# Four pads that shift SBUF buffers by 128 to 384 bytes in a two-layer hybrid encoder

## The chip, the cores and the metric

The kernel runs on one core of a Trainium2 chip. The metric is the device time of one execution, in microseconds (us). Every run of the kernel before took between 1643.23 and 1654.07 us, with a median of 1650.0 us over three runs. TensorE is called PE in the rows, and its weight loads PEld; VectorE is DVE, ScalarE is ACT, GpSimd is POOL, and SP is the queue that issues most transfers.

## The reference

The reference is an encoder trunk of two layers on 512 positions of width 1024, in float32. Layer 0 mixes with dilated window attention and chunked gated linear attention; layer 1 mixes with a bidirectional state-space layer and a convolution module. Each layer then has cross-attention into 256 memory tokens and a gated feed-forward block with a depthwise convolution of width 3:

```python
def reference(...):
    h = x
    for layer in range(DEPTH):              # DEPTH = 2
        i = layer // 2
        hn = rmsnorm(h, g_mix[layer])
        if layer % 2 == 0:
            h = h + mixer_ab(hn, ...)        # attention and gated linear attention
        else:
            h = h + mixer_cd(hn, ...)        # S5 state space and Conformer convolution
        memn = rmsnorm(mem, g_mem[layer])
        h = h + cross_attention(rmsnorm(h, g_xattn[layer]), memn, ...)
        h = h + conv_ffn(rmsnorm(h, g_ffn[layer]), ...)
    return rmsnorm(h, g_final)

def conv_ffn(hn, w_up, w_conv, b_conv, w_down):
    u = depthwise_conv(hn @ w_up, w_conv, b_conv)      # width 1024 -> 2 * 2816
    val, gate = jnp.split(u, 2, axis=-1)
    return (jax.nn.silu(gate) * val) @ w_down          # width 2816 -> 1024
```

Nearly all of the arithmetic is in dense products: the projections of the mixers, the four of the cross-attention, and `w_up` and `w_down`.

## The kernel before

**Activations.** Features lie on the 128 partitions and the 512 positions along the free axis. The residual stream is eight tiles `h[c]`, each 128x512 float32. To keep float32 accuracy, each operand of a dense product is held as two parts of type float32r: `hg[c]`, 128x2x512, holds the high part of the normed stream in `hg[c][:, 0]` and what is left of it in `hg[c][:, 1]`. The same shape is used for the outputs of the mixers (`oa`, `ob`, and `cm`, `at`, `bm`, `cst` in layer 1), of the cross-attention (`ox`), and for the gated product of the feed-forward block (`g`).

**Weights.** A block of weights, 128x1024 float32, is brought by one DMA into `wr` (line 140). ScalarE copies it to `wh` as float32r (line 194), and VectorE (GpSimd for some blocks, lists `LPOOL` and `XPOOL`) computes the rest `wl` (line 195). Then TensorE runs, for each of the block's eight chunks of 128 columns, three matmuls (`mm3`, lines 199 to 201): high by high, high by low, low by high. Each of them loads 128x128 weights into the array and streams a moving operand of 512 columns past them. So a block is 24 matmuls, and each of these has a weight load of its own; PE's instructions come in the fixed sequence load, matmul, load, matmul.

**Order of work.** A scheduler lays out the instructions of each engine when the kernel is built. In the mixers and the cross-attention PE's order is also pinned by hand (`pinned`, `XSEQ`, `CD`), and small float32 matmuls and transposes stand between the blocks. In the feed-forward block (`ffn`) the order is `up` for the 22 chunk pairs and `down` for three groups of them (`GROUPS`), almost all of it full blocks: `up` has `hg` as moving operand, `down` has `g`. During layer 0's feed-forward block GpSimd and VectorE also compute parameters of layer 1's state-space part (`tick`, `s5_params`).

**Buffers.** SBUF is given out by pools in the order in which the pools and their tiles are opened: `P` ("keep") for what lives throughout, `WP` for `wr`, `wh` and `wl`, and one pool for each stage (`T`, `TG`, `TA`, `TM`, `TP`). A tile that is allocated earlier moves the later ones of the same side up by its size. In the program as built, `hg` starts in each partition at a place that leaves 480 when divided by 512 bytes, and the weight buffers `wh` and `wl` leave 352. Chunks within a block and halves within a tile lie 512 or 2048 bytes apart, so that the remainder is the same for a whole buffer. The remainders of the others stand in the table in the section on the change. "Distance" below is the start of the weights that are loaded beside a matmul, less the start of that matmul's moving operand, modulo 512 bytes: for `hg` with `wh` it is 352 - 480 = 384.

Of the kernel before, what the change touches and what calls it, by code (L numbers as in the profile page):

```python
# [11 lines left out]
F32 = mybir.dt.float32  # L12
# [78 lines left out]
def trunk(ctx, tc, xT, memT, pos, vec, amask, cmask, bmask,  # L91
# [4 lines left out]
    P = ctx.enter_context(tc.tile_pool(name="keep", bufs=1))  # L96
# [6 lines left out]
    def nm(p):  # L103
        n_[0] += 1
        return f"{p}_{n_[0]}"
# [15 lines left out]

    h = [P.tile([128, S], F32, tag=f"h{c}", bufs=1, name=f"h{c}") for c in range(NC8)]
    hg = [P.tile([128, 2, S], F32R, name=f"hg{c}") for c in range(NC8)]

    def mm_ps():
        return PS.tile([128, 512], F32, tag="mm", bufs=4, name=nm("mm"))
# [71 lines left out]
    def mm3(ps, lH, lL, rH, rL, start, stop):  # L198
        PE.matmul(ps, lH, rH, start=start, stop=False)  # L199
        PE.matmul(ps, lH, rL, start=False, stop=False)  # L200
        PE.matmul(ps, lL, rH, start=False, stop=stop)  # L201
# [96 lines left out]
    def mixer_ab(nnext, eskv):  # L298
        es = ExitStack()
        T = es.enter_context(tc.tile_pool(name="m0", bufs=1))  # L300

        def b2(tag, bufs, pool=None):
            return (pool or T).tile([128, S], F32, tag=tag, bufs=bufs, name=nm(tag))
# [405 lines left out]
        TM = es.enter_context(tc.tile_pool(name="m0m", bufs=1, side="right"))  # L709
        mg = [TM.tile([128, 2, S], F32R, name=f"mg{i}") for i in range(4)]  # L710
        TA = es.enter_context(tc.tile_pool(name="m0a", bufs=1))
        o_a = [TA.tile([128, 2, S], F32R, name=f"oa{i}") for i in range(4)]
        def ptrans(t, j, p_):
            tp = tp_ps()
            for jt in range(4):
                PE.transpose(tp[:, 128 * jt:128 * jt + 128], p_[:, 128 * jt:128 * jt + 128], ident)  # L716
            pt = b2("pt", 3, TA)
            if j % 2 == 0:
                A.activation(pt, tp, AF.Copy)
            else:  # L720
                V.tensor_copy(pt, tp)
            return pt

        def pv(t, j, pt):
# [6 lines left out]
            if j == 7:  # L731
                den = pair[t][1]
                V.reciprocal(den, den)
                on = b2("on", 1, TA)
                V.tensor_tensor(on.rearrange("p (j d) -> p j d", d=64), onat.rearrange("p (j d) -> p j d", d=64),
# [210 lines left out]
    def ffn(l, norm, nnext, start=None, tick=lambda n: None):  # L946
# [3 lines left out]
        if start is not None:  # L950
            start()
# [108 lines left out]
    def s5_angles(T):  # L1060

        def sm(tag):
            return T.tile([128, 64], F32, name=nm(tag))

        lam = T.tile([128, 3, 64], F32, name="lam")
        nc.sync.dma_start(lam, s5v)
        lr, li, dt = lam[:, 0], lam[:, 1], lam[:, 2]
        tact(dt, dt, AF.Exp)
        x, th, den, t1, t2, t3 = sm("x"), sm("th"), sm("den"), sm("t1"), sm("t2"), sm("t3")
        mul(x, lr, dt)  # L1070
        mul(th, li, dt)
        mul(den, lr, lr)
        mul(t1, li, li)
        add(den, den, t1)
        V.reciprocal(den, den)

        tact(t1, x, AF.Tanh, scale=0.5)
        G.tensor_scalar(t2, t1, -1.0, 1.0, op0=ALU.mult, op1=ALU.add)
        V.reciprocal(t2, t2)
        mag, em1 = sm("mag"), sm("em1")  # L1080
        G.tensor_scalar(mag, t1, 1.0, None, op0=ALU.add)
        mul(mag, mag, t2)
        G.tensor_scalar(em1, t1, 2.0, None, op0=ALU.mult)
        mul(em1, em1, t2)

        G.tensor_scalar(t1, th, 1.0 / TWO_PI, MAGIC, op0=ALU.mult, op1=ALU.add)
        G.tensor_scalar(t1, t1, -MAGIC, None, op0=ALU.add)
        for cst in (PI2_A, PI2_B, PI2_C):
            G.tensor_scalar(t2, t1, -cst, None, op0=ALU.mult)
            add(th, th, t2)  # L1090
        G.tensor_scalar(th, th, PI_F, -PI_F, op0=ALU.min, op1=ALU.max)
        sn, cs, c1 = sm("sn"), sm("cs"), sm("c1")
        tact(sn, th, AF.Sin)
        tact(c1, th, AF.Sin, scale=0.5)
        A.activation(t1, th, AF.Abs)
        tact(cs, t1, AF.Sin, scale=-1.0, bias=hpi_c)
        return sm, lr, li, x, th, den, t1, t2, t3, mag, em1, sn, cs, c1
# [152 lines left out]
    def mixer_cd(norm, nnext, kv):  # L1250
        es = ExitStack()
        T = es.enter_context(tc.tile_pool(name="m1", bufs=1))
# [15 lines left out]
        for j in range(2):  # L1268
            G.memset(vg[j][:, :, 0:2], 0.0)
            G.memset(vg[j][:, :, 66:68], 0.0)  # L1270
        uT, At, Rg, X, cm, tab, rot = {}, {}, {}, {}, {}, {}, {}

        part, done_ = {}, set()
# [304 lines left out]
    def dump():  # L1578
        for c in range(NC8):
            nc.sync.dma_start(out[c], h[c])  # L1580

    n1 = Norm("g_xattn0")
    eskv = ExitStack()
    kv0 = mixer_ab(n1, eskv)
    if upto == 0:
        return dump()
# [6 lines left out]
    with tc.tile_pool(name="s5p", bufs=1) as TP:  # L1593
        angles, todo, clock = [], [], [0]

        def start():
            angles.append(s5_angles(TP))
            todo.append(s5_params(TP, angles[0]))

        def tick(n):  # L1600

            clock[0] += n
            if clock[0] >= S5_EVERY:
                clock[0] -= S5_EVERY
                next(todo[0], None)

        ffn(0, n2, n3, start, tick)
        for _ in todo[0]:
            pass
        if upto == 2:  # L1610
            return dump()
    n4 = Norm("g_xattn1")
    eskv = ExitStack()
    kv1 = KV(1, eskv)
    mixer_cd(n3, n4, kv1)
    if upto == 3:
        return dump()
# [106 lines left out]
```

## Time and profile before

| | us |
|---|---|
| median of three runs | 1650.0 |
| lowest and highest run | 1643.23, 1654.07 |
| the profiled execution | 1640.53 |
| span of its trace, first to last instruction | 1638.7 |
| PE busy in the span | 1585.5 (97%) |
| PEld busy | 1308.6 (80%) |
| DVE, ACT, POOL busy | 1081.1, 708.1, 366.4 |

The time outside the span is 1.8 us. The mean granted clock of TensorE is 0.988 of the full 2.4 GHz. The profile shows a matmul from its start to its modelled end, and the next one starts before that end; so the mean duration of a matmul (398 ns for those of 512 columns with `hg`) is not what one of them costs in a stream. What one costs is the step from a start to the next start: the length of an undisturbed stretch divided by the matmuls that start in it.

### The profile page before, as it was taken

Reading aid. Unit: us, or ns where it says so; the run is one execution under the profiler, and the core shown is the slowest. Engines: PE = TensorE matmul, PEld = TensorE weight load, DVE = VectorE, ACT = ScalarE, POOL = GpSimd, SP = SyncE. Lnnn points to the kernel's source line nnn. Section 1 sums busy time; section 2 is a strip of 40 time slices with the busy share of each in tenths; the row PEclk is TensorE's granted clock in tenths of the full one; section 3 lists DMA queues with packets and bytes.
Section 4 is the critical chain, followed back from the end, with each engine's and each line's share of the span. In section 5 each row is a group of like instructions: output and inputs, shape, how many; then the busy total and the mean of one; then the engine's idle time right before and its main releaser. Section 6 shows DMA issues by size and latency. Waiting matters only on the chain.

```text
span 1638.7 us, 20958 instructions
## 1 busy us (share of the span) xinstructions
PE 1585.5 (97%) x8036; PEld 1308.6 (80%) x8036; DVE 1081.1 (66%) x1475; ACT 708.1 (43%) x1089; POOL 366.4 (22%) x371
## 2 busy tenths in 40 slices
PE   8999999999999999999999899989999999999997
PEld 6788889888877777877887777878888888888887
DVE  7576766466578899389655997275745766636644
ACT  6464755344444433234335233364534434414423
POOL 8411000000079844444500101230000101100101
PEclk9999999999999999999999899999999999999999
DMA  5322334131222335435544573542302323332231
GB/s 175 108 76 91 117 95 138 52 116 52 74 90 78 121 122 161 135 109 169 148 147 150 181 280 121 201 172 88 103 29 81 100 94 100 90 102 91 82 112 64
DMA packets 76117, 189.11 MB, mean 115 GB/s; under 512 B 8368, under 2 KB 27440, under 8 KB 76016
## 3 DMA queue, kind: packets, MB, share of 16 engines
q1 hardware_dynamic: 75376, 186.58, 35.4%
q8 instruction: 63, 1.03, 0.3%
q0 software_dynamic: 320, 1.05, 0.2%
q14 instruction: 38, 0.31, 0.1%
q10 hardware_dynamic: 320, 0.13, 0.0%
HBM read 162.43 MB, written 19.01 MB: 111 GB/s over the span
## 4 chain that ended last, share of the span: by engine, by line
PE 73%; DVE 12%; POOL 6%; issue 3%; ACT 3%; DMA 3%; SPq 1%; DVEq 0%; ACTq 0%; POOLq 0%
PE mm L201 20%; PE mm L199 20%; PE mm L200 20%; DVE wl L195 2%; PE mm L729 2%; DVE t L963 1%; PE sc L1480 1%; DVE dv L1454 1%; DVE t L964 1%; PE tp L1365 1%; PE tp L716 1%; DVE u L960 1%; POOL t L1131 1%; DVE t L968 1%; POOL wl L195 1%
## 5 line engine op out<-in xcount | busy, mean ns | idle before, releaser
L194 ACT ACTIVATE wh<-wr 128x1024 fp32r<-128x1024 f32 (+1 forms) x229 | 238.9, 1044 | 432.6 <-PE mm L200 349.4
L201 PE MATMUL mm<-hg,wl 128*128 128x512 f32 x1000 | 397.7, 398 | 13.0 <-DVE wl L195 12.6
L199 PE MATMUL mm<-hg,wh 128*128 128x512 f32 x1000 | 402.4, 402 | 0.3 <-ACT wh L194 0.3
L200 PE MATMUL mm<-hg,wh 128*128 128x512 f32 x1000 | 397.1, 397 | 0.0
L195 DVE TENSOR_TENSOR wl<-wr,wh 128x1024 fp32r<-128x1024 f32 (+1 forms) x215 | 279.7, 1301 | 69.6 <-ACT wh L194 67.6
L201 PEld LDWEIGHTS mm<-hg,wl 128*128 128x128 f32 x1000 | 189.5, 190 | 62.6 <-DVE wl L195 16.1
L199 PEld LDWEIGHTS mm<-hg,wh 128*128 128x128 f32 x1000 | 189.6, 190 | 46.8 <-issue 2.2
L200 PEld LDWEIGHTS mm<-hg,wh 128*128 128x128 f32 x1000 | 189.4, 189 | 44.7 <-issue 1.2
L201 PE MATMUL mm<-g,wl 128*128 128x512 f32 x324 | 127.5, 394 | 2.2 <-DVE wl L195 2.2
L199 PE MATMUL mm<-g,wh 128*128 128x512 f32 x324 | 127.9, 395 | 0.0
L200 PE MATMUL mm<-g,wh 128*128 128x512 f32 x324 | 127.2, 392 | 0.0
L968 POOL TENSOR_TENSOR t<-t,t 128x512 f32<-128x512 f32 x22 | 29.0, 1318 | 431.7 <-ACT t L175 431.7
L960 DVE TENSOR_TENSOR u<-mm,R 128x512 f32<-128x512 f32 x88 | 60.3, 687 | 81.5 <-PE mm L201 81.4
L962 ACT ACTIVATE t<-u,vt 128x512 f32<-128x512 f32 x88 | 71.1, 810 | 52.3 <-DVE u L960 52.0
L978 DVE TENSOR_TENSOR h<-mm,h 128x512 f32<-128x512 f32 x40 | 27.6, 690 | 90.7 <-PE mm L201 90.7
L963 DVE SCALAR_TENSOR_TENSOR t<-u,vt,t 128x511 f32<-128x511 f32 x88 | 77.7, 883 | 3.8 <-ACT t L962 3.8
L964 DVE SCALAR_TENSOR_TENSOR t<-u,vt,t 128x511 f32<-128x511 f32 x88 | 76.7, 872 | 4.0 <-DMA dct<-tr 1.4
L201 PEld LDWEIGHTS mm<-g,wl 128*128 128x128 f32 x324 | 60.9, 188 | 16.6 <-DVE wl L195 2.8
L175 ACT ACTIVATE t<-t 128x512 f32<-128x512 f32 x44 | 27.8, 632 | 101.3 <-DVE t L964 101.3
L200 PEld LDWEIGHTS mm<-g,wh 128*128 128x128 f32 x324 | 60.9, 188 | 13.4
L199 PEld LDWEIGHTS mm<-g,wh 128*128 128x128 f32 x324 | 60.9, 188 | 13.2
L195 POOL TENSOR_TENSOR wl<-wr,wh 128x1024 fp32r<-128x1024 f32 x14 | 35.0, 2504 | 136.6 <-ACT wh L194 111.8
(522 smaller groups left out, 3036.4 us busy)
## 6 DMA issues: line engine op xcount, KB each, us to landing
wr<-in_w_up SPq DMA_DIRECT2D x88, 512.0 KB
wr<-in_w_dn SPq DMA_DIRECT2D x32, 448.0 KB
wr<-in_w_ab SPq DMA_DIRECT2D x16, 512.0 KB
wr<-in_w_xv SPq DMA_DIRECT2D x16, 512.0 KB
wr<-in_w_xk SPq DMA_DIRECT2D x16, 512.0 KB
wr<-in_w_xq SPq DMA_DIRECT2D x16, 512.0 KB
wr<-in_w_xo SPq DMA_DIRECT2D x16, 512.0 KB
wr<-in_w_dn SPq DMA_DIRECT2D x16, 512.0 KB
```

Of the source, the lines that this page charges most:

```text
L175: tabbed(A.activation(dst, src, fn, **kw))
L194: A.activation(H[:, :n], raw[:, :n], AF.Copy)
L195: (eng or V).tensor_tensor(L[:, :n], raw[:, :n], H[:, :n].bitcast(F32), ALU.subtract)
L199: PE.matmul(ps, lH, rH, start=start, stop=False)
L200: PE.matmul(ps, lH, rL, start=False, stop=False)
L201: PE.matmul(ps, lL, rH, start=False, stop=stop)
L729: PE.matmul(onat[:, 64 * j:64 * j + 64], pt[:, 128 * jt:128 * jt + 128], va[:, jt, 64 * hd:64 * hd + 64], start=jt == 0, stop=jt == 3)
L960: V.tensor_tensor(u, ps, R, ALU.mult)
L962: A.activation(t, u, AF.Identity, scale=vc(f"cw{l}", 44 + i), bias=vc(f"cb{l}", i))
L963: V.scalar_tensor_tensor(t[:, 1:], u[:, :S - 1], vc(f"cw{l}", i), t[:, 1:], op0=ALU.mult, op1=ALU.add)
L964: V.scalar_tensor_tensor(t[:, :S - 1], u[:, 1:], vc(f"cw{l}", 88 + i), t[:, :S - 1], op0=ALU.mult, op1=ALU.add)
L968: (V if l == 0 else G).tensor_tensor(res[1], res[1], res[0], ALU.mult)
```

## The change

A helper `pad` allocates a tile of so many bytes in a partition and leaves it unused. It is called four times: 128 bytes in `P` after `hg`, 384 bytes in `TA` ahead of `oa`, 192 bytes in the pool of `mixer_cd`, and 320 bytes in `TP`, which lies ahead of the feed-forward tiles of layer 0. No instruction reads or writes a pad.

```diff
     h = [P.tile([128, S], F32, tag=f"h{c}", bufs=1, name=f"h{c}") for c in range(NC8)]
     hg = [P.tile([128, 2, S], F32R, name=f"hg{c}") for c in range(NC8)]
+
+    def pad(pool, n):
+        pool.tile([128, n // 4], F32, name=nm("pad"))
+
+    pad(P, 128)
...
         TA = es.enter_context(tc.tile_pool(name="m0a", bufs=1))
+        pad(TA, 384)
         o_a = [TA.tile([128, 2, S], F32R, name=f"oa{i}") for i in range(4)]
...
             G.memset(vg[j][:, :, 66:68], 0.0)
+        pad(T, 192)
         uT, At, Rg, X, cm, tab, rot = {}, {}, {}, {}, {}, {}, {}
...
             angles.append(s5_angles(TP))
             todo.append(s5_params(TP, angles[0]))
+            pad(TP, 320)
```

On all five engines the instructions stand in the same order, name for name, and wait for the same semaphores as before. What differs is where buffers start. The starts modulo 512 bytes, from the two programs as built:

| buffer | role in a matmul of 512 columns | before | changed |
|---|---|---|---|
| `hg` | moving; weights in `natural` | 480 | 480 |
| `wh`, `wl`, and `xh`, `xl` of the cross-attention | weights; moving in `natural` and `vstep` | 352 | 480 |
| `mg` | weights | 480 | 480 |
| `g`, layer 0 | moving | 32 | 480 |
| `g`, layer 1 | moving | 352 | 480 |
| `ob`, `ox` | moving | 352 | 480 |
| `oa` | moving | 480 | 480 |
| `cm`, `at`, `bm`, `cst` | moving | 160 | 480 |
| `pT` with weights `vn` | moving, weights | 480, 480 | 96, 96 |

PE's order has 5395 places at which a float32r matmul of 512 columns is followed by the weight load of another one. Counted by distance they are:

| distance | 0 | 128 | 192 | 256 | 320 | 384 |
|---|---|---|---|---|---|---|
| before | 1052 | 389 | 144 | 0 | 567 | 3243 |
| changed | 5373 | 10 | 0 | 8 | 0 | 4 |

## Rows read from the trace of the kernel before

**Rows 1.** The page: span, busy time of each engine, share of the last chain.
```profile
span 1638.7 us, 20958 instructions
PE 1585.5 (97%) x8036; PEld 1308.6 (80%) x8036; DVE 1081.1 (66%) x1475; ACT 708.1 (43%) x1089; POOL 366.4 (22%) x371
...
PE 73%; DVE 12%; POOL 6%; issue 3%; ACT 3%; DMA 3%; SPq 1%; DVEq 0%; ACTq 0%; POOLq 0%
```

**Rows 2.** The page's costliest groups: matmuls with hg and g; busy, mean, idle before.
```profile
L199 PE MATMUL mm<-hg,wh 128*128 128x512 f32 x1000 | 402.4, 402 | 0.3 <-ACT wh L194 0.3
L200 PE MATMUL mm<-hg,wh 128*128 128x512 f32 x1000 | 397.1, 397 | 0.0
...
L199 PE MATMUL mm<-g,wh 128*128 128x512 f32 x324 | 127.9, 395 | 0.0
```

**Rows 3.** Timeline in layer 1's feed-forward block: start, duration, engine, line, operation.
```profile
1425.69 0.40 PE L199 MATMUL mm<-hg,wh 128*128 128x512 f32 x1
1425.69 0.19 PEld L200 LDWEIGHTS mm<-hg,wh 128*128 128x128 f32 x1
1425.92 0.39 PE L200 MATMUL mm<-hg,wh 128*128 128x512 f32 x1
1425.93 0.19 PEld L201 LDWEIGHTS mm<-hg,wl 128*128 128x128 f32 x1
```

**Rows 4.** PE by stretch: from:to, length, busy (matmuls), granted clock, DMA share, GB/s.
```profile
418.86:451.77 32.91, 32.91 (x146) 1.00 0.31 97
459.62:531.25 71.63, 71.63 (x308) 1.00 0.27 89
830.22:864.52 34.30, 34.30 (x148) 1.00 0.48 156
1265.60:1426.59 160.99, 160.99 (x691) 1.00 0.30 95
1426.59:1470.13 43.54, 43.54 (x193) 1.00 0.31 97
1470.13:1548.53 78.40, 78.40 (x337) 1.00 0.28 91
1548.53:1601.13 52.60, 52.60 (x233) 1.00 0.36 106
```

**Rows 5.** The same view of three short streams.
```profile
54.00:59.10 5.10, 5.10 (x23) 1.00 0.30 103
67.40:78.09 10.69, 10.69 (x47) 1.00 0.44 113
411.07:415.85 4.78, 4.78 (x22) 1.00 0.00 0
```

**Rows 6.** Groups by shape on PE over the whole span.
```profile
L200 PE MATMUL mm<-wl,hg 128*128 128x512 f32 x64 | 25.9, 405 | 0.7 <-DVE wl L195 0.7
...
L201 PE MATMUL mm<-wh,hg 128*128 128x512 f32 x64 | 25.0, 394 | 0.0
...
L199 PE MATMUL mm<-wh,hg 128*128 128x512 f32 x64 | 24.4, 404 | 0.2 <-ACT wh L194 0.2
...
L200 PE MATMUL mm<-pT,vn 128*128 128x512 f32 x24 | 9.0, 389 | 0.0
```

**Rows 7.** PE by stretch: two streams of matmuls of 256 columns.
```profile
249.44:252.05 2.61, 2.61 (x24) 1.00 0.33 126
...
1606.20:1619.51 13.31, 13.31 (x113) 1.00 0.01 1
```

**Rows 8.** All engines by stretch: length, PE, PEld, DVE, ACT, POOL busy, granted clock.
```profile
560.00:650.00 90.00, 83.72 (x377) 67.13 (x375) 81.51 (x104) 36.62 (x53) 46.40 (x28) 0.98 0.45 135
710.00:790.00 80.00, 73.43 (x333) 59.19 (x332) 74.50 (x98) 31.82 (x47) 38.24 (x23) 0.98 0.44 134
870.00:950.00 80.00, 72.68 (x372) 59.94 (x371) 64.08 (x92) 32.80 (x51) 7.45 (x4) 0.91 0.53 184
950.00:1050.00 100.00, 89.89 (x585) 76.48 (x585) 65.23 (x87) 36.30 (x55) 16.67 (x7) 0.97 0.55 190
```

**Rows 9.** Who waited for whom: waits in us, times, longest.
```profile
PE mm L201 <- DVE wl L195: 15.4, 9, 3.8
```

## The prediction

> **What bounds the kernel.** I read the engines' busy time and the chain of waits first. PE is busy for 1585.5 of 1638.7 us, and 73% of the chain that ended last is PE work [rows 1]. The costliest groups are dense matmuls of 512 columns, three lines of 1000 each with `hg` and of 324 each with `g` as moving operand [rows 2], and PE waited for nothing ahead of most of them. So the price of one such matmul in a stream sets the time. The mean durations of 395 to 402 ns [rows 2] are not that price, since a matmul begins before the modelled end of the one before. The timeline shows the step: starts at 1425.69 and 1425.92, and the load of the next weights begins within 10 ns of each matmul [rows 3]. What PE reads together is therefore a matmul's moving operand and the weights of the next.
>
> **The step depends on the distance, in the trace of before.** I took undisturbed stretches, all at granted clock 1.00, the full 2.4 GHz, and divided each by its matmuls [rows 4]. The count of each stretch holds one matmul that began ahead of its left edge, so one is taken off.
>
> - `hg` in three stretches, distance 384: 71.63/307, 160.99/690 and 78.40/336 us, 233.3 ns each time.
> - `g` in layer 0, distance 320: 34.30/147, 233.3 ns.
> - `g` in layer 1, distance 0: 43.54/192 and 52.60/232, 226.8 and 226.7 ns.
> - `ox` in the cross-attention, distance 0: 32.91/145, 227.0 ns.
>
> The two stretches of `g` do the same work from the same weight buffers, and differ in where the moving operand lies. In layer 1 `hg` and `g` alternate four times without a pause, and the step goes 233.3, 226.8, 233.3, 226.7. The DMA share, 0.27 to 0.48, doesn't sort them: it is 0.36 in the stretch of 226.7 and 0.28 in one of 233.3. So the change's claim is visible before it is made: 6.5 ns less per matmul at distance 0, in a long stream.
>
> **The change, part by part.** No instruction is added, removed or moved. The pads' effect is on distances: of 5395 places where one matmul of 512 columns follows another, 4343 have a distance other than 0 now, and 22 afterwards. At some 150 of the 4343 PE waits for something first, and I count no gain there: 4193 are left.
>
> *Long streams.* The four of [rows 4] at distance 384 or 320 hold 307 + 690 + 336 + 147 = 1480 matmuls. At 6.5 ns: 9.6 us.
>
> *The other 2713* stand in shorter streams, between small matmuls, transposes and waits. Short streams of `hg` now take 5.10/22 = 231.8 and 10.69/46 = 232.4 ns; a short one of `ox` at distance 0 takes 4.78/21 = 227.6 ns [rows 5]. So one gains 4.2 to 4.8 ns in streams as short as these and 6.5 in long ones. I take 5.2, nearer to the short end, because most of these streams are 20 to 50 matmuls: 14.1 us. The upper bound is 6.5 (17.6 us). The lower is 3, if the streams between waits are too broken to settle (8.1 us).
>
> *The 1052 places at distance 0 now* stay there: nothing. *Matmuls of 256 columns* (`mg` moving, 384 of them) go from distance 384 to 0 too. A stream at 384 takes 2.61/22 = 118.6 ns and one at 0 takes 13.31/111 = 119.9 [rows 7] (here two began early), so these lose 1.3 ns each, about 0.5 us. *Small float32 matmuls and transposes* change distance as well; the half-width ones bound them at 1.3 ns for the some 1900 that are left, 2.5 us either way, and I take 0.
>
> *What is hidden again.* A gain ahead of a wait for another engine is lost if that engine doesn't get faster. In two stretches of layer 0's feed-forward block DVE is busy for 81.51 of 90 and 74.50 of 80 us, and PE waits [rows 8]; the waits of PE for DVE's `wl` are 15.4 us in all, at 9 places [rows 9]. Some 550 of the 4193 matmuls lie in those stretches, 2.9 us of gain at 5.2 ns. In the state-space mixer, 870 to 1120 us, PE also has holes and the granted clock is 0.91 and 0.97 in [rows 8]; 440 matmuls, 2.3 us. If all of it is absorbed, 5.2 us; I take half, 2.6, because DVE's work on each chunk starts from a PE result and moves forward with it.
>
> Sum: 9.6 + 14.1 - 0.5 - 2.6 = 20.6 us. Bounds: 9.6 + 8.1 - 0.5 - 5.2 - 2.5 = 9.5 and 9.6 + 17.6 - 0.5 + 2.5 = 29.2. The profiled execution took 1640.5 us, of which 1638.7 is span; it would take 1619.9. It stands 9.5 below the median of the runs shown, 1650.0, and under the lowest of them. I expect the gain to be the same in every run, since it sits in each matmul: **1629.4 us**, 1.25% faster.
>
> **A rule that speaks against it.** The rows show 233.3 and 226.8 ns for the same work at two places of its operand [rows 4]. The Trainium skill, page "TensorE: Matmul & The Clock Gate", section "Part 2: What happens when you issue a matmul", says that TensorE has two independent read ports into SBUF, so that loading the next weights takes no read bandwidth from the running matmul. By that, no placement of the two operands could matter, and the gain would be 0 instead of 20.6 us. The trace doesn't agree, by its 6.5 ns.
>
> **Rivals.**
>
> 1. *No effect.* The steps of 226.8 ns come from something that goes with the stage, and placement has no part in it. For: `g` at 233.3 and at 226.8 are in different layers, and `ox` is a third place. Against: `hg` in layer 0 and in layer 1 has the same 233.3, with VectorE, GpSimd and the transfers differently loaded. The time would be 1650.0, or 1640.5 for an execution like the profiled one. The page's rule above would give this time. Chance 0.1.
>
> 2. *Absorbed.* The faster stream reaches VectorE's weight preparation more often, the waits of [rows 9] grow in layer 0's feed-forward block and in both mixers, and the holes bring the clock's half level back more often. For: DVE at 81.51 of 90 us [rows 8]. Against: in layer 1's feed-forward block, a third of the gain, PE runs 160.99 us without a hole [rows 4]. Gain 5 to 15 us: 1635 to 1645, centre 1640. Chance 0.15.
>
> 3. *Slower: the place, not the distance.* The fast streams, `g` in layer 1 and `ox`, have their moving operand at 352; `hg` at 480 and `g` of layer 0 at 32 are slow. If 480 is a slow place for a moving operand, the pads bring nothing to `hg` and move the 1052 fast ones from 352 to 480: 1052 x 6.5 = 6.8 us slower, 1656.8. It decides as soon as the place counts for more than the distance. Against: weights as moving operand lie at 352 too, at distance 128, and have mean durations of 394 to 405 ns, as `hg` has; `pT` at 480 with its weights at 480 has 389 [rows 6]. Chance 0.05.
>
> That the pads don't move what they should is no rival: the starts of the changed program are known.
>
> **Chances and range.** The forecast, a gain of 15 to 29 us, has 0.7. Faster or slower by over 1%, 16.5 us, is about what can be told from no change. The forecast's centre is only 4 us beyond that bound and the runs of before spread over 11 us, so I count 0.9 of the forecast, a fifth of rival 2 and little else as faster by over 1%: 0.67. Within 1%: 0.29, from rivals 1 and 2 and most of 3. Slower by over 1%: 0.04, rival 3 in a slow set of runs. The range runs from 1616 (a gain of 29 and a set of runs 5 us under the median shown) to 1643, which takes in rival 2 up to near its end and leaves 0.2 outside.
>
> **What would show it.** In the changed profile: `hg` in the long stretch of layer 1 steps at 226.8 ns, `g` in layer 0 too; `g` in layer 1 and `ox` stay at 226.7 to 227.0; the mean duration of the `hg` matmuls falls by several ns from 397 to 402; matmuls of 256 columns rise from 118.6 towards 119.9; the waits of PE for `wl` grow by no more than 3 us. The prediction is wrong in its first step if `hg` stays at 233.3 with distance 0, and in its sum if the step falls but PE's idle time rises by as much.

## The result, and the profile after

The changed kernel took 1631.39 us, the median of six runs (1627.70 to 1635.04), against 1649.11 for six of the kernel before (1643.23 to 1654.07): a ratio of 0.9895 with a 95% interval of 0.987 to 0.9919. That is 17.7 us less. Two further sets of runs, on other occasions, gave 0.9931 (0.9909 to 0.9954, below as e3) and 0.9931 (0.9908 to 0.9954, e10). So the gain is real, and it is 0.7 to 1.05%, according to the set. The changed kernel's medians in the three sets lie within 3.6 us of each other (1631.39, 1632.67, 1634.98); the kernel before had 1649.11 in the first set, and 1643.2 and 1645.5 in the other two. The size of the gain hangs mostly on that.

The profiled execution took 1632.09 us, of which 1630.3 is span. Lines 199 to 201 are now 206 to 208. The page's busy times and the groups that answer to [rows 1] and [rows 2]:

```profile
span 1630.3 us, 20958 instructions
PE 1570.0 (96%) x8036; PEld 1313.0 (81%) x8036; DVE 1079.4 (66%) x1475; ACT 707.4 (43%) x1089; POOL 368.2 (23%) x371
...
L206 PE MATMUL mm<-hg,wh 128*128 128x512 f32 x1000 | 398.3, 398 | 2.0 <-ACT wh L201 2.0
L207 PE MATMUL mm<-hg,wh 128*128 128x512 f32 x1000 | 392.8, 393 | 0.0
```

The mean durations with `hg` fell by 4 ns. The step shows it plainly. The same undisturbed stretches as in [rows 4], PE alone (from:to, length, busy with the number of matmuls, granted clock, DMA share, GB/s; again one matmul of each count began ahead of the left edge):

```profile
415.54:448.45 32.91, 32.91 (x146) 1.00 0.29 97
456.12:525.72 69.60, 69.60 (x308) 1.00 0.27 91
827.06:860.42 33.36, 33.36 (x148) 1.00 0.50 160
1264.01:1420.42 156.41, 156.41 (x691) 1.00 0.31 98
1420.42:1463.94 43.52, 43.52 (x193) 1.00 0.31 97
1463.94:1540.10 76.16, 76.16 (x337) 1.00 0.30 94
```

`hg` now steps by 69.60/307, 156.41/690 and 76.16/336 us, 226.7 ns each time where it was 233.3, and `g` of layer 0 by 33.36/147, 226.9 ns, where it was 233.3. `ox` and `g` of layer 1, which had distance 0 before, take 227.0 and 226.7 as before (the second stretch of `g`, not shown, too).

But the span fell by only 8.4 us between the two profiled executions, and PE's busy share fell too. I laid the two traces side by side, matmul by matmul (PE's order is the same), and sorted the differences of the steps. At 5186 places between matmuls of 512 columns that are undisturbed in both traces the steps lost 22.9 us. At places that lie in a stretch at the clock's half level in either trace 8.1 us came back, and 6.3 us at waits and other disturbed places. No view prints these sums; they are worked out from the starts of the matmuls in the two traces. The stretches in which it came back, all engines (length; PE, PEld, DVE, ACT, POOL busy; granted clock, DMA share, GB/s), answer to [rows 8]:

```profile
480.00:560.00 80.00, 76.74 (x343) 63.07 (x342) 63.45 (x68) 32.53 (x44) 75.67 (x110) 0.98 0.35 109
560.00:650.00 90.00, 80.46 (x369) 65.61 (x367) 80.61 (x103) 36.16 (x53) 44.17 (x27) 0.98 0.43 129
710.00:795.00 85.00, 78.14 (x353) 63.68 (x353) 76.10 (x99) 33.03 (x49) 46.36 (x29) 0.96 0.47 141
...
950.00:1060.00 110.00, 98.18 (x629) 83.70 (x629) 65.52 (x85) 36.92 (x57) 19.07 (x8) 0.92 0.56 194
```

PE has holes in all four. POOL is nearly full in the first, and DVE in the second and third; in the last neither is. The granted clock is 0.98, 0.98, 0.96 and 0.92. Before, the first of these stretches had 79.48 us of PE and a clock of 1.00, and the last a clock of 0.97; the second had 0.98 already [rows 8]:

```profile
480.00:560.00 80.00, 79.48 (x353) 64.00 (x352) 67.24 (x73) 34.73 (x46) 75.58 (x113) 1.00 0.35 109
710.00:795.00 85.00, 78.43 (x363) 63.45 (x362) 78.45 (x102) 35.13 (x52) 40.68 (x27) 0.98 0.45 134
...
950.00:1060.00 110.00, 99.89 (x670) 85.96 (x670) 69.77 (x91) 39.06 (x59) 19.02 (x8) 0.97 0.56 196
```

POOL is busy for 75.6 us of the first 80 in both: its chain of state-space parameters does not get shorter when PE's matmuls do. The last stretch varies from trace to trace: its clock was 0.95 and 0.97 in two further traces of the changed kernel (e3 and e10), so what came back there is not shown to be of the change.

### The profile page after: what moved, and what is told of

Same layout as the page of the kernel before. It is cut to its first block, busy times and chain, and to the rows that moved or that the text cites. A ratio compares the mean times of both kernels' runs of the same rounds, so it can differ in the third digit from the quotient of the medians.

```text
span 1630.3 us, 20958 instructions
## 1 busy us (share of the span) xinstructions
PE 1570.0 (96%) x8036; PEld 1313.0 (81%) x8036; DVE 1079.4 (66%) x1475; ACT 707.4 (43%) x1089; POOL 368.2 (23%) x371
## 3 DMA queue, kind: packets, MB, share of 16 engines
q0 software_dynamic: 320, 1.05, 0.2%
## 4 chain that ended last, share of the span: by engine, by line
PE 69%; DVE 13%; POOL 6%; DMA 3%; issue 3%; ACT 3%; SPq 1%; ACTq 0%; DVEq 0%; POOLq 0%
PE mm L208 20%; PE mm L206 19%; PE mm L207 19%; DVE wl L202 2%; PE mm L737 2%; PE sc L1489 1%; DVE t L972 1%; DVE dv L1463 1%; DVE t L971 1%; PE tp L724 1%; PE tp L1374 1%; POOL t L1139 1%; POOL wl L202 1%; DVE tr L1138 1%; PE sc L206 1%
## 5 line engine op out<-in xcount | busy, mean ns | idle before, releaser
L201 ACT ACTIVATE wh<-wr 128x1024 fp32r<-128x1024 f32 (+1 forms) x229 | 239.1, 1044 | 419.7 <-PE mm L207 316.8
L208 PE MATMUL mm<-hg,wl 128*128 128x512 f32 x1000 | 393.7, 394 | 13.8 <-DVE wl L202 13.4
L206 PE MATMUL mm<-hg,wh 128*128 128x512 f32 x1000 | 398.3, 398 | 2.0 <-ACT wh L201 2.0
L207 PE MATMUL mm<-hg,wh 128*128 128x512 f32 x1000 | 392.8, 393 | 0.0
L208 PEld LDWEIGHTS mm<-hg,wl 128*128 128x128 f32 x1000 | 189.7, 190 | 57.5 <-DVE wl L202 16.2
L207 PEld LDWEIGHTS mm<-hg,wh 128*128 128x128 f32 x1000 | 189.8, 190 | 40.0 <-issue 1.2
L208 PE MATMUL mm<-g,wl 128*128 128x512 f32 x324 | 126.7, 391 | 2.4 <-DVE wl L202 2.4
L207 PE MATMUL mm<-g,wh 128*128 128x512 f32 x324 | 126.2, 389 | 0.0
L968 DVE TENSOR_TENSOR u<-mm,R 128x512 f32<-128x512 f32 x88 | 60.3, 687 | 74.2 <-PE mm L208 74.0
L208 PEld LDWEIGHTS mm<-g,wl 128*128 128x128 f32 x324 | 60.8, 188 | 16.1 <-DVE wl L202 3.2
L207 PEld LDWEIGHTS mm<-g,wh 128*128 128x128 f32 x324 | 60.9, 188 | 12.4
```

Of the source, the lines that this page charges most:

```text
L201: A.activation(H[:, :n], raw[:, :n], AF.Copy)
L968: V.tensor_tensor(u, ps, R, ALU.mult)
```

## The experiments

### e1: the step by distance alone

```diff
-    (the encoder)
+    def stream(letter, moving, weights, cols=512, reps=4):
+        ps = PS.tile([128, 512], F32, tag=f"b{n % 8}", bufs=1, name="q" + letter)
...
+        todo = [(8 * r + c, k) for r in range(reps) for c in range(8) for k in range(3)]
+        for i, (c, k) in enumerate(todo):
+            a, b = weights + 128 * (c % 8), moving + 512 * (k == 1)
+            PE.matmul(ps[:, :cols], w[:, int(k == 2), a:a + 128], x[:, b:b + cols], ...)
```

> Only streams of 96 matmuls, each with its own weight load, from one weight tile and one moving tile; the encoder is left out. Streams differ in the distance of weights and moving operand modulo 512 bytes (every 32 bytes from 0 to 480, and 16, 48, 496), four more have distance 0 at other places (32, 128, 256 and 384 bytes on), and four have 256 columns. Theory, distance modulo 512: about 226.8 ns a matmul at distance 0, at all five places; about 233 ns at 128, 192, 320 and 384; at 256, which no stream of the kernel before had, 233 as well. Rival, modulo 256: 226.8 at 256 too. Rival, the place counts: the streams at distance 0 differ among each other by 6 ns, and distances with the same moving place don't matter. Rival, independent ports: all streams the same within 1 ns. At 256 columns: about 119.9 at 0 and 118.6 at 384.

Measured: the timeline of PE, one row for each stream of 96 matmuls (start, duration, engine, line, operation). `qda` to `qdp` have distances 0, 32, 64 and so on to 480; `qpa` is a second place with distance 0, and `qha`, `qhb`, `qhc` have 256 columns and distances 0, 128 and 256. A start less the start before it, over 96, is the step.

```profile
35.11 21.92 PE L118 MATMUL qda<-x,w 128*128 128x512 f32 x96
56.87 22.56 PE L118 MATMUL qdb<-x,w 128*128 128x512 f32 x96
79.28 22.55 PE L118 MATMUL qdc<-x,w 128*128 128x512 f32 x96
101.67 22.65 PE L118 MATMUL qdd<-x,w 128*128 128x512 f32 x96
124.16 22.48 PE L118 MATMUL qde<-x,w 128*128 128x512 f32 x96
146.47 22.58 PE L118 MATMUL qdf<-x,w 128*128 128x512 f32 x96
168.89 22.14 PE L118 MATMUL qdg<-x,w 128*128 128x512 f32 x96
190.87 22.57 PE L118 MATMUL qdh<-x,w 128*128 128x512 f32 x96
213.27 21.96 PE L118 MATMUL qdi<-x,w 128*128 128x512 f32 x96
235.07 22.56 PE L118 MATMUL qdj<-x,w 128*128 128x512 f32 x96
...
458.62 21.95 PE L118 MATMUL qpa<-x,w 128*128 128x512 f32 x96
480.41 21.98 PE L118 MATMUL qpb<-x,w 128*128 128x512 f32 x96
...
545.76 11.68 PE L118 MATMUL qha<-x,w 128*128 128x256 f32 x96
557.28 11.55 PE L118 MATMUL qhb<-x,w 128*128 128x256 f32 x96
568.67 11.66 PE L118 MATMUL qhc<-x,w 128*128 128x256 f32 x96
```

| distance | 0 | 32 | 64 | 96 | 128 | 160 | 192 | 224 | 256 |
|---|---|---|---|---|---|---|---|---|---|
| step, ns | 226.7 | 233.4 | 233.2 | 234.3 | 232.4 | 233.5 | 229.0 | 233.3 | 227.1 |

From 256 on the row repeats: 288 to 448 gave 233.3, 233.2, 234.3, 232.4, 233.5 and 229.0 ns. Distances 16, 48 and 496 gave 233.3, 234.7 and 231.6. The other places at distance 0 gave 226.8 to 227.2. So the distance decides and the place does not, as the theory had it; but the period is 256 bytes, not 512: my expectation of 233 at 256 was wrong, and the rival with 256 was right. Distance 192, that is 64 bytes short of a period, is a second, smaller dip. At 384 the stream here takes 232.4 ns, where `hg` in the kernel took 233.3 at the same distance; no run explains these 0.9 ns. At 256 columns the order is reversed, 120.0 ns at 0 and 118.6 at 128, as [rows 7] had it.

### e9: the period in the kernel itself

```diff
         T = es.enter_context(tc.tile_pool(name=f"f{l}", bufs=1))
+        if l == 1:
+            pad(T, 64)
...
-            pad(TP, 320)
+            pad(TP, 64)
```

(and a pad of 384 or 448 bytes in the cross-attention's pool)

> The changed kernel with other pads for g: distance 256 in layer 0 (320 bytes become 64) and 448 in layer 1 (64 more in its pool); a pad in the cross-attention puts ox at a mixture of distances. hg stays at 0. By the streams alone (e1), with a period of 256 bytes: g of layer 0 about 227.1 ns a matmul, g of layer 1 about 229.0, hg 226.8. Rival, a period of 512 as the change's words have it: g of layer 0 about 233.

Measured, PE by stretch: `g` of layer 0 at distance 256, `hg` at 0, `g` of layer 1 at 448:

```profile
838.01:871.37 33.36, 33.36 (x148) 1.00 0.49 160
1270.54:1426.95 156.41, 156.41 (x691) 1.00 0.30 98
1426.95:1470.91 43.96, 43.96 (x193) 1.00 0.30 96
```

33.36/147 is 226.9 ns, 156.41/690 is 226.7 and 43.96/192 is 229.0: the values of e1 for 256, 0 and 448 to 0.2 ns. The period of 256 bytes holds in the kernel. The time of its single run, 1639.61 us, decides nothing.

### e4 and e8: another place, and the first pad alone

```diff
+    pad(P, 128)
     hg = [P.tile([128, 2, S], F32R, name=f"hg{c}") for c in range(NC8)]
...
     pad(P, 128)
```

> The changed kernel with 128 more bytes ahead of hg, so that nearly all operands start at 96 instead of 480 modulo 512 and the distances stay 0 (221 places go to 384, where mg, which lies on the other side of SBUF, meets the shifted tiles). Theory, distance: 226.8 ns in the long streams, the time of the changed kernel within 3 us (221 x 6 ns is 1.3 us). Rival, place: the streams change by several ns, and the time by more than 10 us.

Measured: 1632.17 us, ratio 0.9926 (0.9899 to 0.9954), as the changed kernel beside it in the same set (0.9931). `hg` at 96 instead of 480 steps by 156.41/690, 226.7 ns; the rival of the place is out:

```profile
1268.64:1425.05 156.41, 156.41 (x691) 1.00 0.30 98
```

e8 keeps the first pad and leaves out the others (shown against the changed kernel):

```diff
     pad(P, 128)
...
-        pad(TA, 384)
...
-        pad(T, 192)
...
-            pad(TP, 320)
```

> The first pad alone (128 bytes after hg). 4566 places have distance 0; g of layer 0 stays at 320 (519 places), cm, at, bm and cst have 192, oa 384. Theory: streams of hg, of ox and of g in layer 1 at 226.8 ns, g of layer 0 at 233.3; 519 x 6.5 = 3.4 us of the gain are missing, so the time is 2 to 4 us above the changed kernel. Rival (place): more than 10 us from it.

Measured: 1634.72 us, ratio 0.9936 (0.9921 to 0.9951). The stretches of `g` in layer 0 and of `hg` in layer 1:

```profile
834.23:868.53 34.30, 34.30 (x148) 1.00 0.48 156
1270.59:1427.00 156.41, 156.41 (x691) 1.00 0.30 98
```

`g` of layer 0 is back at 34.30/147, 233.3 ns, and `hg` has kept its 226.7. The undisturbed places against a trace of before gain 18.7 us instead of the 22.3 of e3, 3.6 less, as expected. In the time the difference to the changed kernel is within the intervals: the first pad alone brings nearly all that can be measured.

### e2 and e3: both kernels again

No edit.

> The kernel before once more, for a second trace of it. Theory: streams at distance 384 and 320 take 233.3 ns again and the median is 1649 us; if the first trace of before had fewer waits and less of the half clock than usual, this one shows a span nearer to 1647 and a granted clock below 0.988, with the difference in the waits between 480 and 1120 us. Rival: the trace is as before, span 1639 and clock 0.988, and then waits and the half clock were added by the change.

> The changed kernel once more. Theory: 226.8 ns in the long streams, median 1631 us, waits and granted clock (0.98) that vary from trace to trace by some 5 us. Rival (waits added by the change): the same places wait by the same amounts again, against the second trace of before.

Measured: before 1645.47 us in this set of its own (ratio to the reference runs 1.0009, 0.9998 to 1.002) and 1643.2 for those; changed 1632.67, ratio 0.9931. Who waited for whom on PE from about 480 to 1120 us (us in all, times, longest), in the second trace of before:

```profile
PE mm L201 <- DVE wl L195: 14.9, 8, 4.0
...
PE mm L200 <- DVE wl L195: 1.3, 1, 1.3
...
PE sc L1192 <- POOL o L1235: 0.4, 1, 0.4
```

and in the second trace of the changed kernel:

```profile
PE mm L208 <- DVE wl L202: 15.4, 7, 4.1
...
PE sc L1200 <- POOL o L1243: 2.7, 1, 2.7
...
PE mm L207 <- DVE wl L202: 2.2, 1, 2.2
```

The wait for POOL's `o` is 2.7 or 2.8 us in every trace that has the pad after `hg` and the steps at their old place (the first of the changed kernel, e3, e10, e4, e8, e9), and 0.4 in both of before. So my theory that the waits are chance was wrong here; the rival, that the change adds them, has it. The waits for `wl`, 16.2 us in all before and 17.6 after, hardly grew. The small matmul that waits, in the first trace of before and in this one (start, duration; in brackets the hole ahead of it), and two matmuls of 512 columns after it:

```profile
554.94 1.29 PE L1192 MATMUL sc<-bb,o 128*128 128x16 f32 x10 [0.44 <-POOL o L1235]
```

```profile
551.24 3.41 PE L1200 MATMUL sc<-bb,o 128*128 128x16 f32 x16 [2.75 <-POOL o L1243]
...
555.06 0.63 PE L207 MATMUL mm<-hg,wh 128*128 128x512 f32 x1
555.49 0.63 PE L208 MATMUL mm<-hg,wl 128*128 128x512 f32 x1
```

PE comes to this matmul at 548.5 us instead of 554.5, 6.0 us earlier; GpSimd has the product ready at 551.2 instead of 554.9, only 3.7 us earlier. What follows, PE by stretch in this trace (length, busy, granted clock):

```profile
548.00:552.00 4.00, 1.25 (x8) 0.93 0.23 66
552.00:556.00 4.00, 4.00 (x17) 0.50 0.88 238
556.00:560.00 4.00, 4.00 (x14) 0.71 0.47 160
```

and in the first trace of before:

```profile
548.00:552.00 4.00, 4.00 (x18) 1.00 0.29 120
552.00:556.00 4.00, 3.56 (x21) 1.00 0.25 70
556.00:560.00 4.00, 4.00 (x23) 1.00 0.93 253
```

After a hole of 2.75 us the granted clock falls to 0.50, the level of 1.2 GHz, and matmuls of 512 columns step by 0.43 us instead of 0.23. Before, with a hole of 0.44 us ahead of the same matmul, it stayed at 1.00. All six traces with the longer hole have the half level set in within 3 us of its end, and neither trace of before has. By the pairing of matmuls, 3.8 us came back between 540 and 560 us in the first pair of traces and 4.6 in this one. The same pairing as above, e2 against e3: 22.3 us gained at undisturbed places, 8.4 lost at the half level, 2.1 at the rest; 11.8 remain.

### e5 and e6: without GpSimd's long products, in both kernels

```diff
-                    G.tensor_tensor(o1, ex(x0), pw(pr), ALU.mult)
-                    G.tensor_tensor(o2, ex(x1), pw(pi_), ALU.mult)
-                    G.tensor_tensor(o1, o1, o2, op)
+                    G.memset(o1, 0.0)
```

> The kernel before, with GpSimd's three large products for each of the state-space tables (lines 1233 to 1235) replaced by one fill with zeros, so that GpSimd's chain beside layer 0's feed-forward block is much shorter. The tables are then zero; PE's work is the same. Theory (the change's gain is swallowed where PE waits for GpSimd and for VectorE, which GpSimd slows): PE's waits for DVE's wl, 15 us before, fall to a few us and the kernel to 1615 to 1632 us. Rival (waits come from elsewhere): time and waits within 5 us of the kernel before.

> The same cut in the changed kernel. Theory: the difference between the two kernels without GpSimd's products is the whole gain of the streams, 21 to 25 us (1.3 to 1.5%), instead of 10.5 us on this kind of run with them, and the share of the half clock is the same in both. Rival (the gain is lost at random, or to the half clock whatever the waits): the difference stays at 10 to 18 us, with more half clock in the changed one.

Measured: 1628.86 us for the kernel before with this cut, ratio 0.9898 (0.9883 to 0.9913), and 1611.45 for the changed one, 0.9805 (0.9782 to 0.9829). The waits of PE for DVE's `wl` fell from 17.4 and 18.7 us in the first traces (lines L200 and L201 together, L207 and L208 in the changed kernel) to under 4 in both, and the longest of VectorE's subtractions from 480 to 800 us from 3.1 to 1.4 us (shortest, median and longest in ns, before and e5), so it was GpSimd's work that held VectorE up:

```profile
L195 DVE TENSOR_TENSOR wl<-wr,wh x51: 1082/1225/3111, 482.3 to 798.7; 128x1024 fp32r<-128x1024 f32 x46, 128x896 fp32r<-128x896 f32 x5
```

```profile
L195 DVE TENSOR_TENSOR wl<-wr,wh x54: 1091/1225/1417, 480.3 to 794.9; 128x1024 fp32r<-128x1024 f32 x47, 128x896 fp32r<-128x896 f32 x7
```

All engines in one stretch, the kernel before and then the changed one, both with this cut:

```profile
560.00:650.00 90.00, 90.00 (x423) 73.81 (x423) 65.68 (x109) 39.15 (x57) 15.36 (x23) 1.00 0.47 146
```

```profile
560.00:650.00 90.00, 90.00 (x428) 75.06 (x427) 63.13 (x107) 38.61 (x56) 13.55 (x20) 1.00 0.51 153
```

No hole is left here, nor from 710 to 795 us, the clock is 1.00 in both, and the gain stays where it is made. Between the two traces the span falls by 24.6 us (1628.2 to 1603.6), 23.3 of it at undisturbed places, at mean clocks of 0.986 and 0.987. The medians, however, differ by only 17.4 us, less than the theory's 21 to 25 and in the rival's 10 to 18: of six runs of the changed one three had a clock of 0.986 to 0.988 and took 1605 to 1608 us, three had 0.980 or 0.981 and took 1615 to 1619, while the four of the other all had 0.986 or 0.987. So part of the loss to the half clock is there without GpSimd's waits. Where it falls in the runs at 0.980 stays open: the trace of e6 is of the run at 0.987.

### e7, e11 and e12: the state-space steps six ticks later

```diff
-        angles, todo, clock = [], [], [0]
+        angles, todo, clock = [], [], [-6]
```

> The changed kernel with the state-space steps begun six ticks later (clock from -6), so that PE reaches the first of their small matmuls after GpSimd is done. Theory: the wait of that matmul for POOL o, 2.7 us after the change and 0.4 before, goes, with the half clock that follows it; 2 to 5 us below the changed kernel. Rival (the waits only move on to later places, since GpSimd's and VectorE's chains are what bounds that stretch): within 2 us of the changed kernel.

> The changed kernel beside the next two on one chip. 0.9895 and 0.9931 of before so far; 0.989 to 0.994 expected by all theories.

> The changed kernel with the state-space steps six ticks later, again. Theory (the wait for GpSimd that the faster streams brought is the one removed): 2 to 5 us below e10. Rival (the difference between chips made it look faster): within 2 us of e10.

> The six ticks in the kernel before, without pads. Theory: there PE waited for GpSimd at this place for only 0.4 us, so the time is within 2 us of before. Rival (the later steps help by themselves, whatever the streams do): as much below before as e11 is below e10.

| kernel | us | ratio to before, 95% interval |
|---|---|---|
| e7, changed and later | 1626.80 | 0.9883 (0.9864 to 0.9902) |
| e10, changed | 1634.98 | 0.9931 (0.9908 to 0.9954) |
| e11, changed and later | 1621.52 | 0.9854 (0.9826 to 0.9881) |
| e12, before and later | 1637.56 | 0.9953 (0.9934 to 0.9972) |

e10 to e12 ran on one chip; e7's set has no run of the changed kernel. The later steps take 13.5 us off the changed kernel there, far more than the 2 to 5 that I expected. In e11's trace PE doesn't wait for POOL's `o` any more, and its waits for DVE's `wl` are shorter, against 16.0 in e10's:

```profile
PE mm L208 <- DVE wl L202: 9.9, 9, 4.4
```

But the theory of e12 was wrong: the same edit takes 7.9 us off the kernel before, where that one wait was 0.4 us. Its trace has shorter waits for `wl` too (10.9 us), but it is of one of e12's two longest runs, 1641.63 us, no shorter than the traces of before, so where the 7.9 us come from is not shown. The six ticks help by themselves. That they help more beside the pads is not shown: the intervals of 0.9953 and of 0.9854 over 0.9931 overlap. Read the other way, the pads take 16.0 us off where the steps are later (1637.56 to 1621.52) and 10.5 where they are not (1645.5 to 1634.98). e11 is the fastest version here that computes all of it, and it beats both kernels.

## Why the prediction was right, point by point

- **The step depends on the distance.** Right, and the size was right: 233.3 to 226.7 ns in four long stretches, and e1, e4 and e9 leave no other cause among the rivals. The first rival, no effect, and with it the rule of two independent read ports that the prediction cites from the Trainium skill, would have left `hg` at 233.3. The trace of before had already decided this, by two stretches of `g` that differ in little else. What I did not see there is the period: no stream of 512 columns had distance 256, so that 256 and 512 could not be told apart. Why the distance counts, and why with this period, no run shows.
- **The gross sum.** 9.6 + 14.1 was forecast for the matmuls of 512 columns, 23.7; 22.9 and 22.3 us were measured at undisturbed places in two pairs of traces. The half-width matmuls go the way of [rows 7], 118.6 against 120.0 ns in e1; in the kernel they lost about half of the 0.5 us that I took off for them, and the small ones changed by next to nothing, as taken.
- **What is hidden again.** This is the term that was mis-sized. I took 2.6 us and bounded it at 5.2, the gain that lies in the stretches themselves. Measured: 22.9 less 17.7 in the first set, 5.2, and about 12 in the others; PE's idle time in the span rose from 53.2 to 60.3 us between the first two traces. It exceeds my bound in two sets of three because the stretches do not only swallow their own gain. PE reaches the wait for POOL's `o` earlier, waits longer in one piece, and comes out of it at the half clock, and then takes longer over matmuls that it had at the full clock before. My sum had no price for that wait and none for the clock; the wait that I had pointed at, for `wl`, hardly grew. I had named such a loss as the second rival, with a chance of 0.15 and a gain of 5 to 15 us. The first set, 17.7, lies in the forecast; the other two, 10.5 by the medians, lie in the rival. Both mechanisms were at work at once, and I had set them against each other instead of adding them. That the first set came out so near to the forecast is in part luck.
- **The clock.** The mean granted clock of the runs was 0.9837 before (56 runs of four sets; the first set has no clock on record for that kernel) and 0.9803 after (21 runs of three). The difference, 0.0034 of 1632 us, is 5.5 us by this estimate, about half of what came back.
- **The place.** 1656.8 us by the third rival. The changed kernel has `hg` at 226.7 ns at 480, the place that the rival called slow, and e4 shows 0.9926 with nearly all operands at another.
- **The profiled execution of before** stood 9.5 us below its median, and I took the gain from the median. That gave 1629.4, close to the measured 1631.39; but the high median was the unusual number. Four later sets of the kernel before had medians of 1643.2 to 1645.5, and its second profiled execution took 1641.24. For an execution like the profiled one the same sum gave 1619.9, and it took 1632.09: the pairs of traces differ by 8.4 and 11.8 us, not by 20.6. That the gain is the same in every run was wrong.

## What to carry to other kernels

Where a long stream of matmuls with a weight load each is the bound, work out from the buffers' starts how far the next weights lie from the moving operand, and look for two stretches in the trace at hand that differ in that alone: they price the change before it is made. Then ask for each stretch who else is nearly full there. A gain on the bound engine is kept where that engine runs without holes, is swallowed where another chain has a fixed length, and can turn into a loss where the longer hole brings the half clock, as it did at one place here.

## What was not expected of the hardware

- The step of a matmul of 512 float32r columns depends on the distance with a period of 256 bytes: 226.7 to 227.1 ns at 0 and 256, 229.0 at 192 and 448, and 231.6 to 234.7 at all others that e1 tried.
- The best distance for 512 columns is the slower one for 256 columns, 120.0 ns against 118.6.
- A hole of 2.75 us on PE was followed by a granted clock of 0.50 in six traces; one of 0.4 us at the same place of the program was not, in two.
